# The low part of every fourth weight tile, made by a copy on ACT and an adding transfer

## The chip, the cores and the metric

The kernel runs on one core of a Trainium2 chip. A core has a matrix engine (PE, with a weight loader PEld beside it), a vector engine (DVE), a scalar engine (ACT), a general engine (POOL) and a queue engine (SP). Transfers run on 16 DMA engines, whichever queue issues them; here almost all are issued from SP's queue, and POOL's own queue is used twice. The metric is the device time of one execution in microseconds, smaller is better.

## The reference

The program is a decoder trunk on 256 tokens of width 2048, in float32. There are two layers. The first mixes by latent attention (8 heads) and matrix memory (4 heads) behind one input projection and one output projection; the second by dilated sliding-window attention (16 heads). Each is followed by an MLP of width 8192 with a squared ReLU, and a final RMS norm ends it. Nearly all of the work is products of 256 tokens with weight matrices, some 400 MB of float32 that are each used once.

```
x = x + mix
x = x + squared_relu_mlp(rms_norm(x, norm_mlp[layer]), mlp_w1[layer], mlp_w2[layer])
```

## The kernel before

The matrix engine takes a reduced float32 format, so that every operand is split into a high part of 12 bits and a low part, the rest, and a product is made of three partial products: high by high, high by low, low by high.

The weights come in 769 tiles, counted by `n_w` from 1 in the order of use. `weights` (L93 to L109) makes one: SP issues the transfer of the raw tile (L104), ACT rounds it into `hi` (L107, tile `wh` in the trace), and DVE subtracts (L108, `wl`). Raw, high and low tiles lie in rings of four buffers each, so that tile n uses the buffers of tile n-4. ACT can write `wh` of tile n when PE has done its last product with tile n-4, and DVE then writes `wl`; SP can load the raw tile n+4 when both have read tile n. 716 of the tiles have 128 x 1024 elements (512 KB); those of the input projection at the start are smaller (364, 360 or 344 KB).

`mm_tokens` (L111 to L117) uses a tile with the tokens on the output's partitions: three products for each of two token blocks and each 128 rows, the second of them with the low part. `mm_feats` (L119 to L122) has the features on the partitions: one product of 512 columns with the high part, then one of 256 with the low. So the low part is wanted by the second product of a tile.

The stages in order, with PE's names for their outputs: the input projection of the first layer (`c` tiles 1 to 25, `r`, `qk`, `v`) with the latent heads' projections in between (`un`, `ur`, `uk`, `uv`, one tile each for a pair of heads, four times), its output projection (`o`), the first MLP (tiles 130 to 385: 32 tiles `h`, then 32 tiles `y`, four times), the second layer (`q`, `k`, `v`, `o`), and the second MLP. In its last part (`finish`) the last four tiles are used by products `z` (L863 to L865), for one token block after the other.

The order of the instructions of each engine is made by a planner out of the program's order and its own estimate of times, then fixed; an engine works through its list in order. POOL has little in its list: two norms' powers for whole layers, one for the latents, two in the end, and the transfers of a table (L707) and of the final gain (L828).

Of the kernel before, what the change touches and what calls it, by code (L numbers as in the profile page):

```python
# [14 lines left out]
P = 128  # L15
# [14 lines left out]
def _shape_constants():  # L30
    """Identity, triangles, additive masks and rotary tables: functions of the shapes alone."""
    f = np.float32
    r = np.arange(P)
    ident = np.eye(P, dtype=f)
    cum = (r[:, None] <= r[None, :]).astype(f)
    tri = np.where(r[None, :] <= r[:, None], 0.0, BIG).astype(f)
    zero = np.zeros((P, P), f)
    causal = np.concatenate([tri, zero, tri], 1)
    causal_t = np.concatenate([tri.T, zero, tri.T], 1)

    def log_count(d):
        c = ((d >= 0) & (d <= 128)).astype(int) + ((d >= 0) & (d % 4 == 0)) + ((d >= 0) & (d % 16 == 0))
        return np.where(c > 0, np.log(np.maximum(c, 1)) / DIL_SCALE, BIG).astype(f)

    d0 = r[:, None] - r[None, :]
    dil = np.concatenate([log_count(d0), log_count(d0 + P), log_count(d0)], 1)

    def angles(dim):
        half = dim // 2
        inv = f(THETA) ** (-np.arange(half, dtype=f) * f(2.0) / f(dim))  # L50
        ang = np.arange(S, dtype=f)[:, None] * inv[None, :].astype(f)
        return np.cos(ang), np.sin(ang)

    def by_token(t):
        return t.reshape(NB, P, -1).transpose(1, 0, 2).reshape(P, -1)

    cos, sin = angles(64)
    c64, s64 = by_token(np.concatenate([cos, cos], 1)), by_token(np.concatenate([-sin, sin], 1))
    qc, qs = np.concatenate([cos.T] * 4, 0), np.concatenate([sin.T, sin.T, -sin.T, -sin.T], 0)
    cos, sin = angles(128)  # L60
    oc, os_ = np.concatenate([cos.T, cos.T], 0), np.concatenate([sin.T, -sin.T], 0)
    first = np.concatenate([ident, cum], 1)
    even = np.concatenate([causal, causal_t, c64, s64, qc, qs], 1)
    odd = np.concatenate([dil, oc, os_], 1)
    return tuple(np.ascontiguousarray(t, dtype=f) for t in (first, even, odd))
# [3 lines left out]
def trunk(ctx: ExitStack, tc: tile.TileContext, plan, a, c_first, c_even, c_odd, out):  # L69
# [20 lines left out]

# [1 line left out]
    n_w = [0]  # L92

    def weights(w, k0, kt, c0, n):
        """Rows k0*128.. (kt blocks of 128), columns c0..c0+n (or the ranges c0 of columns, n in all)
        of matrix w -> hi, lo in SBUF.
        The matrix lies in DRAM tile after tile in the order of use: plan says which."""
        name, layer, row = w
        stream, tiles = plan[name, layer]
        at = sum(t[1] * t[3] for t in tiles) * P  # L100
        tiles.append((row + k0 * P, kt, c0 if isinstance(c0, tuple) else ((c0, n),), n))
        n_w[0] += 1
        raw = wpool.tile([P, kt, n], F32, name=f"wr{n_w[0]}", tag="raw", bufs=4)
        nc.sync.dma_start(raw, stream[at:at + P * kt * n].rearrange("(p k n) -> p k n", k=kt, n=n))  # L104
        hi = wpool.tile([P, kt, n], FR, name=f"wh{n_w[0]}", tag="hi", bufs=4)
        lo = wpool.tile([P, kt, n], FR, name=f"wl{n_w[0]}", tag="lo", bufs=4)
        nc.scalar.activation(hi, raw, AF.Copy)  # L107
        nc.vector.tensor_tensor(lo, raw, hi.bitcast(F32), OP.subtract)  # L108
        return hi, lo  # L109

    def mm_tokens(accs, n, T, hi, lo, first, last):  # L111
        """accs[b][:, :n] += T_b.T @ (hi + lo), tokens on the output's partitions."""
        for b in range(NB):
            xh, xl = T[:, 0, b * P:(b + 1) * P], T[:, 1, b * P:(b + 1) * P]
            nc.tensor.matmul(accs[b][:, :n], xh, hi, start=first, stop=False)  # L115
            nc.tensor.matmul(accs[b][:, :n], xh, lo, start=False, stop=False)  # L116
            nc.tensor.matmul(accs[b][:, :n], xl, hi, start=False, stop=last)  # L117

    def mm_feats(ac, T, hi, lo, first, last):  # L119
        """ac[:, :256] + ac[:, 256:] += (hi + lo).T @ T, features on the output's partitions."""  # L120
        nc.tensor.matmul(ac, hi, T.rearrange("p a t -> p (a t)"), start=first, stop=False)  # L121
        nc.tensor.matmul(ac[:, :S], lo, T[:, 0, :], start=False, stop=last)  # L122

    def steps_tokens(Ts, w, c0, n, evac, kt=2, order=None, name="a", split_first=False):
        """Steps (closures) of Ts.T @ w[:, c0:c0+n]; evac(accs) at the end."""
        order = list(order if order is not None else range(len(Ts)))
# [19 lines left out]
    def steps_feats(Ts, w, c0, evac, n=256, name="f"):  # L146
        """Steps of (w[:, c0:c0+n]).T @ Ts; evac(f, acc) for its blocks of 128 features."""
        box = {}
# [18 lines left out]
    def both(pool, out, ac, name):  # L167
        """out = the two halves of a product by features, together."""
        t = pool.tile([P, S], F32, name=f"bt_{name}", tag="bt", bufs=2)
        nc.scalar.activation(t, ac[:, S:], AF.Copy)  # L170
        nc.vector.tensor_add(out, ac[:, :S], t)  # L171

    def rotate(pool, out, y, cos, sin, name):
        """out = y turned: its features i and 64 + i are a pair; sin is negative in the second half."""
        u = pool.tile([P, S], F32, name=f"ro_{name}", tag="ro", bufs=2)
# [6 lines left out]
    def split_to(T, src, scale=None):  # L182
        """T = hi, lo of src * scale (src [128, 256] float32, scale a column or None)."""
        if scale is None:
# [6 lines left out]

# [1 line left out]
    x = [[xpool.tile([P, 512], F32, name=f"x{b}{c}") for c in range(4)] for b in range(NB)]  # L193
# [17 lines left out]

# [1 line left out]
    class Norm:  # L213
# [10 lines left out]
        def load(self, ks):  # L224
            """k-tiles ks (of one pair) from x as it comes, laid out with the features first;
            in the tile that x itself comes into later."""
            n, g, j0 = len(ks), ks[0] // 2, ks[0] % 2
# [19 lines left out]
        def close(self):  # L247
            """mean(x*x) + eps, of a token."""
            s = const.tile([P, NB], F32, name=f"s_{self.name}", tag="s_sum", bufs=2)
            nc.vector.tensor_reduce(s, self.ss, mybir.AxisListType.X, OP.add)  # L250
            nc.vector.tensor_scalar(self.var, s, 1.0 / D, EPS, OP.mult, OP.add)
# [10 lines left out]

# [1 line left out]
    def attn_scores(pool, ps, mask, scale, name):  # L264
        """ps [128, 384]: block 0 x keys 0..127, block 1 x keys 0..255."""
        s = pool.tile([P, 384], F32, name=f"s_{name}", tag="s", bufs=2)
# [27 lines left out]
    def attn_out(pT, v0, v1, name):  # L294
        """out.T [dv, tokens], split: v0, v1 [128 keys, 128]."""
        ps = mis(f"po_{name}")
# [6 lines left out]
    def token_row(pool, column, name):  # L303
        """[128, 256]: a value per token (column [128, block]) along the free axis, on every partition."""
        ps = mis(name)
# [11 lines left out]
    def weave(main, side):  # L317
        """main steps with the side steps spread over them."""
        done = 0
# [18 lines left out]

# [1 line left out]
    def even_layer(norm):  # L340
# [10 lines left out]

        # MLA latents
        cn = big.tile([P, NB, 1088], F32, name="cn", tag="big")
# [57 lines left out]

        # gates and output gate
        gt = sm.tile([P, NB, 8], F32, name="gt")
# [43 lines left out]
        def rows(src, h, name):  # L457
            """[128, 256]: src[:, b, h] of the tokens along the free axis, on every partition."""
            ps = mis(name)
# [36 lines left out]

        # mLSTM queries and keys: convolution over the tokens, channels on partitions
        QK = {}
# [85 lines left out]

        # MLA heads, two at a time
        QT, KT, QR, V = {}, {}, {}, {}
# [113 lines left out]

# [1 line left out]
    def odd_layer(norm):  # L702
# [86 lines left out]

# [1 line left out]
    def two_chunks(T, w, c, evac, ks):  # L791
        """Chunks c, c+1 together, k-tiles outermost."""
        box = {}
# [31 lines left out]
    def finish(H, wq, evac_y, scale, sm):  # L825
        """The last product into x, and the final norm: a block of tokens after the other."""
        gf = sm.tile([P, D], F32, name="gf")
# [172 lines left out]
```

## Time and profile before

| | |
|---|---|
| runs | 2175.34, 2172.87, 2172.86 us; median 2172.87 |
| span of the profiled execution | 2170.5 us |
| PE busy | 2157.0 us, 99% |
| DVE busy | 1317.7 us, 61% |
| ACT busy | 1033.1 us, 48% |
| POOL busy | 5.1 us |
| moved by transfers | 404.49 MB, mean 186 GB/s |
| granted clock | 0.999 of full speed |

The profiled execution is given by its span alone, from the first to the last instruction; the median of the runs is 2.4 us above it. Ends of products are modelled by the profiler, so that PE's rows overlap; where PE waits is read from rows of waits and from the starts of products.

### The profile page before, as it was taken

To read this page: it belongs to the slowest core of one execution; us is meant where nothing else is said; L and a number is where in the kernel's file an instruction comes from. 1 tells how busy PE (TensorE), PEld (TensorE's weight loads), DVE (VectorE), ACT (ScalarE), POOL (GpSimd) and SP (SyncE) were. 2 spreads that over 40 slices of the span, in tenths; PEclk is the share of its full clock that TensorE was granted. 3 is DMA by queue.
4 is the path that set the end of the run, shared out by engine and by line. 5 is a ranking of instruction groups with operands and counts; after the bars stand their busy time and mean duration, and the time that the engine had idled before them with its cause. 6 is when DMAs were issued, how large, how long until landed. Compare 5 with 4: busy or idle time off the path is not lost.

```text
span 2170.5 us, 29176 instructions
## 1 busy us (share of the span) xinstructions
PE 2157.0 (99%) x11214; PEld 1850.6 (85%) x11214; DVE 1317.7 (61%) x1909; ACT 1033.1 (48%) x1476; POOL 5.1 (0%) x11
## 2 busy tenths in 40 slices
PE   9999999999999999999999999999999999999998
PEld 8988888888888888888888888888888888888887
DVE  5668556655654665565667666556546555655655
ACT  6676445443443443444544444455434434434443
POOL 0000000000000000000000000000000000000000
PEclk9999999999999999999999999999999999999999
DMA  8555555555555555555565545555555565555554
GB/s 294 168 164 173 166 180 180 190 193 194 185 188 193 191 185 194 191 188 186 173 201 168 175 165 181 187 185 186 192 192 188 185 194 191 187 193 188 189 189 143
DMA packets 115131, 404.49 MB, mean 186 GB/s; under 512 B 12912, under 2 KB 13552, under 8 KB 114864
## 3 DMA queue, kind: packets, MB, share of 16 engines
q1 hardware_dynamic: 114624, 401.07, 56.7%
q8 instruction: 87, 1.43, 0.3%
q0 software_dynamic: 224, 1.51, 0.2%
q14 instruction: 52, 0.43, 0.1%
q10 hardware_dynamic: 144, 0.06, 0.0%
HBM read 400.49 MB, written 2.10 MB: 185 GB/s over the span
## 4 chain that ended last, share of the span: by engine, by line
PE 98%; ACT 1%; issue 0%; DVE 0%; DMA 0%; SPq 0%; POOLq 0%; POOL 0%; DVEq 0%; ACTq 0%
PE h L121 22%; PE h L122 11%; PE y L115 11%; PE y L117 11%; PE y L116 11%; PE q L121 3%; PE k L121 3%; PE o L117 3%; PE o L115 3%; PE o L116 3%; PE v L115 2%; PE v L117 2%; PE v L116 2%; PE k L122 1%; PE q L122 1%; PE qk L121 1%
## 5 line engine op out<-in xcount | busy, mean ns | idle before, releaser
L108 DVE TENSOR_TENSOR wl<-wr,wh 128x1024 fp32r<-128x1024 f32 (+4 forms) x769 | 922.1, 1200 | 714.6 <-ACT wh L107 709.8
L107 ACT ACTIVATE wh<-wr 128x1024 fp32r<-128x1024 f32 (+4 forms) x769 | 799.3, 1040 | 928.9 <-PE y L117 382.3
L121 PE MATMUL h<-T,wh 128*128 128x512 f32 x2048 | 721.0, 398 | 0.0
L122 PE MATMUL h<-T,wl 128*128 128x256 f32 x2048 | 572.7, 280 | 0.0
L121 PEld LDWEIGHTS h<-T,wh 128*128 128x128 f32 x2048 | 384.6, 188 | 94.1 <-DVE T L189 0.3
L115 PE MATMUL y<-wh,T 128*128 128x512 f32 (+1 forms) x1024 | 395.2, 386 | 0.0
L116 PE MATMUL y<-wl,T 128*128 128x512 f32 (+1 forms) x1024 | 395.0, 386 | 0.0
L117 PE MATMUL y<-wh,T 128*128 128x512 f32 (+1 forms) x1024 | 395.0, 386 | 0.0
L122 PEld LDWEIGHTS h<-T,wl 128*128 128x128 f32 x2048 | 386.3, 189 | 0.4
L117 PEld LDWEIGHTS y<-wh,T 128*128 128x128 f32 x1024 | 192.3, 188 | 38.8
L115 PEld LDWEIGHTS y<-wh,T 128*128 128x128 f32 x1024 | 192.3, 188 | 38.7
L116 PEld LDWEIGHTS y<-wl,T 128*128 128x128 f32 x1024 | 192.3, 188 | 38.4
L115 PE MATMUL o<-wh,T 128*128 128x512 f32 x256 | 102.3, 400 | 0.0
L117 PE MATMUL o<-wh,T 128*128 128x512 f32 x256 | 99.8, 390 | 0.0
L116 PE MATMUL o<-wl,T 128*128 128x512 f32 x256 | 99.6, 389 | 0.0
L170 ACT ACTIVATE bt_h<-h 128x256 f32<-128x256 f32 x128 | 48.7, 381 | 96.8 <-PE h L122 96.8
L121 PE MATMUL q<-T,wh 128*128 128x512 f32 x256 | 92.3, 403 | 0.0
L121 PE MATMUL k<-T,wh 128*128 128x512 f32 x256 | 92.2, 403 | 0.0
L171 DVE TENSOR_TENSOR hu<-h,bt_h 128x256 f32<-128x256 f32 x128 | 54.0, 421 | 44.5 <-ACT bt_h L170 44.5
L115 PE MATMUL v<-wh,T 128*128 128x512 f32 x192 | 77.4, 403 | 0.0
L117 PE MATMUL v<-wh,T 128*128 128x512 f32 x192 | 74.9, 390 | 0.0
L116 PE MATMUL v<-wl,T 128*128 128x512 f32 x192 | 74.8, 390 | 0.0
(261 smaller groups left out, 2018.6 us busy)
## 6 DMA issues: line engine op xcount, KB each, us to landing
wr<-in_mlp_w SPq DMA_DIRECT2D x512, 512.0 KB, 3.5
wr<-in_od_w_qkv SPq DMA_DIRECT2D x96, 512.0 KB, 3.5
wr<-in_ev_w_in SPq DMA_DIRECT2D x32, 512.0 KB, 3.6
wr<-in_ev_w_out SPq DMA_DIRECT2D x32, 512.0 KB, 3.4
wr<-in_od_w_out SPq DMA_DIRECT2D x32, 512.0 KB, 3.5
wr<-in_ev_w_in SPq DMA_DIRECT2D x24, 344.0 KB, 3.2
wr<-in_ev_w_in SPq DMA_DIRECT2D x15, 364.0 KB, 5.7
wr<-in_mla_w_ukv SPq DMA_DIRECT2D x8, 512.0 KB, 3.6
```

The source lines that it names most:

```text
L107: nc.scalar.activation(hi, raw, AF.Copy)
L108: nc.vector.tensor_tensor(lo, raw, hi.bitcast(F32), OP.subtract)
L115: nc.tensor.matmul(accs[b][:, :n], xh, hi, start=first, stop=False)
L116: nc.tensor.matmul(accs[b][:, :n], xh, lo, start=False, stop=False)
L117: nc.tensor.matmul(accs[b][:, :n], xl, hi, start=False, stop=last)
L121: nc.tensor.matmul(ac, hi, T.rearrange("p a t -> p (a t)"), start=first, stop=False)
L122: nc.tensor.matmul(ac[:, :S], lo, T[:, 0, :], start=False, stop=last)
L170: nc.scalar.activation(t, ac[:, S:], AF.Copy)
L171: nc.vector.tensor_add(out, ac[:, :S], t)
```

## The change

In every tile whose number is a multiple of four (192 of 769), the low part is no longer made by DVE. ACT writes the negative of the rounded raw tile into `lo`, and a transfer issued from POOL's queue adds the raw tile to it, read a second time from DRAM. The other tiles are made as before. Comments and docstrings are left out of the file too; the line count shifts by five behind the edit.

```diff
         nc.scalar.activation(hi, raw, AF.Copy)
-        nc.vector.tensor_tensor(lo, raw, hi.bitcast(F32), OP.subtract)
+        if n_w[0] % 4 == 0:
+            nc.scalar.activation(lo, raw, AF.Copy, scale=-1.0)
+            nc.gpsimd.dma_start(lo, stream[at:at + P * kt * n].rearrange("(p k n) -> p k n", k=kt, n=n),
+                                accum_op=OP.add)
+        else:
+            nc.vector.tensor_tensor(lo, raw, hi.bitcast(F32), OP.subtract)
         return hi, lo
```

## Rows read from the trace of the kernel before

**Rows 1.** The page: busy time by engine, and the chain that ended last

```profile
PE 2157.0 (99%) x11214; PEld 1850.6 (85%) x11214; DVE 1317.7 (61%) x1909; ACT 1033.1 (48%) x1476; POOL 5.1 (0%) x11
...
PE 98%; ACT 1%; issue 0%; DVE 0%; DMA 0%; SPq 0%; POOLq 0%; POOL 0%; DVEq 0%; ACTq 0%
```

**Rows 2.** Waits of PEld: in total us, times, longest

```profile
PEld c L115 <- ACT wh L107: 4.9, 3, 4.3
PEld uk L121 <- DVE QT L171: 1.4, 3, 0.8
PEld c L116 <- DVE wl L108: 1.1, 3, 0.5
```

**Rows 3.** Lines: count | busy us, mean ns | idle before, releasers

```profile
L108 DVE TENSOR_TENSOR wl<-wr,wh 128x1024 fp32r<-128x1024 f32 (+4 forms) x769 | 922.1, 1200 | 714.6 <-ACT wh L107 709.8
L107 ACT ACTIVATE wh<-wr 128x1024 fp32r<-128x1024 f32 (+4 forms) x769 | 799.3, 1040 | 928.9 <-PE y L117 382.3 <-issue 195.8 <-PE h L121 131.0
```

**Rows 4.** Timeline (start, duration us) of one y tile, number 190

```profile
512.69 1.06 ACT L107 ACTIVATE wh<-wr 128x1024 fp32r<-128x1024 f32 x1 [1.66 <-PE y L117]
...
520.65 0.39 PE L115 MATMUL y<-wh,T 128*128 128x512 f32 x1
...
520.87 0.39 PE L116 MATMUL y<-wl,T 128*128 128x512 f32 x1
```

**Rows 5.** Timeline of one h tile, number 212, and ACT after the next

```profile
574.04 1.06 ACT L107 ACTIVATE wh<-wr 128x1024 fp32r<-128x1024 f32 x1 [1.76 <-PE h L121]
...
576.93 1.05 ACT L107 ACTIVATE wh<-wr 128x1024 fp32r<-128x1024 f32 x1
...
577.88 0.38 ACT L170 ACTIVATE bt_h<-h 128x256 f32<-128x256 f32 x1
...
582.63 0.28 PE L122 MATMUL h<-T,wl 128*128 128x256 f32 x1
```

**Rows 6.** Timeline around POOL's transfer of the final gain

```profile
1394.12 1.06 ACT L107 ACTIVATE wh<-wr 128x1024 fp32r<-128x1024 f32 x1 [2.01 <-PE o L117]
...
1395.21 1.22 DVE L108 TENSOR_TENSOR wl<-wr,wh 128x1024 fp32r<-128x1024 f32 x1 [1.78 <-ACT wh L107]
1395.30 0.58 POOL L828 DMA_DIRECT2D gf<-in_norm_final  x1 [325.17 <-ACT wh L107]
```

**Rows 7.** Transfers of 1395 to 1400.5 us: queues, issues, us to landing

```profile
q0 software_dynamic: 144, 1.05, 54.3%
q1 hardware_dynamic: 194, 0.73, 32.4%
...
gf<-in_norm_final POOLq DMA_DIRECT2D x1, 1024.0 KB, 5.1
```

**Rows 8.** All 769 loads of raw tiles

```profile
DMA to landing us min/median/max: 2.5/3.5/7.3
```

**Rows 9.** Timeline of tile 4

```profile
9.79 0.82 ACT L107 ACTIVATE wh<-wr 128x728 fp32r<-128x728 f32 x1 [0.70 <-DMA wr<-in_ev_w_in]
...
10.51 0.89 ACT L188 ACTIVATE T<-x,cols 128x256 fp32r<-128x256 f32 x2
...
11.61 0.43 PE L116 MATMUL c<-wl,T 128*128 128x364 f32 x1
```

**Rows 10.** Stretch 10 to 40 us: engines, clock, DMA share, GB/s

```profile
10.00:40.00 30.00, 29.90 (x179) 29.29 (x178) 18.68 (x29) 23.94 (x46) 0.71 (x1) 1.00 0.96 351
```

**Rows 11.** Timeline of tile 24

```profile
45.62 0.81 ACT L107 ACTIVATE wh<-wr 128x720 fp32r<-128x720 f32 x1 [1.16 <-PE c L117]
...
51.48 0.33 PE L116 MATMUL c<-wl,T 128*128 128x360 f32 x1
```

**Rows 12.** Timeline of two of the four uk tiles, numbers 36 and 68

```profile
71.23 1.06 ACT L107 ACTIVATE wh<-wr 128x1024 fp32r<-128x1024 f32 x1 [0.40 <-ACT T L188]
...
77.56 0.28 PE L122 MATMUL uk<-T,wl 128*128 128x256 f32 x1
...
157.78 1.05 ACT L107 ACTIVATE wh<-wr 128x1024 fp32r<-128x1024 f32 x1
...
163.41 0.28 PE L122 MATMUL uk<-T,wl 128*128 128x256 f32 x1
```

**Rows 13.** Timeline of the end, tile 768

```profile
2148.12 1.06 ACT L107 ACTIVATE wh<-wr 128x1024 fp32r<-128x1024 f32 x1 [1.82 <-PE y L117]
...
2153.80 0.28 PE L864 MATMUL z<-wl,T 128*128 128x256 f32 x1
```

## The prediction, written before the changed kernel was run

> **What bounds the kernel now.** I read the page's busy times and its chain first: PE is busy for 2157.0 of 2170.5 us and makes 98% of the chain that ended last [rows 1]. Then the waits: what the weight loader ever waited for DVE's low parts is 1.1 us, all at the start, and its longest wait of all is 4.3 us for the first tile [rows 2]. DVE sits idle for 714.6 us in front of its subtractions, for ACT; ACT sits idle for 928.9 us in front of its roundings, mostly for PE to give a buffer back [rows 3]. So the low parts are early, and DVE's time is worth nothing as such: what matters is how early each low part is, and how much later the changed ones come. That is read tile by tile from timelines, and it differs by stage.
>
> **How early the low part is wanted.** In a y tile ACT starts to round at 512.69, released by PE's last product with the tile four before; PE wants the low part at 520.87 [rows 4]. The changed tile has a second ACT copy of the same size. ACT's next instruction starts 0.95 us after a rounding does (576.93 to 577.88 [rows 5]), so the second copy ends 0.95 after the first: 512.69 + 1.06 + 0.95 = 514.70. From there to 520.87 are 6.2 us. In an h tile: 574.04 + 1.06 + 0.95 = 576.05, wanted at 582.63: 6.6 us [rows 5]. These two stages have 127 of the 192 changed tiles; in each of them the copy and then the whole trip of the adding transfer have to fit in that.
>
> **What is removed.** 192 subtractions of 1.2 us [rows 3], 230 us of DVE time. PE doesn't wait for them, so this is 0. At most it gives back the waits for DVE that are seen: 1.1 + 1.4 us [rows 2], and I take none.
>
> **What is added on ACT.** 192 copies, each holding the queue for some 0.95 us: 182 us, into 928.9 us of idle time. Behind one stands the next rounding, which has 2.7 us until PE frees its buffer. I cost it at 0 by itself; if ACT were full, each copy would cost its 0.95.
>
> **The trip of the adding transfer.** The trace has no adding transfer. The floor is a plain load of a raw tile: 2.5 us at least, 3.5 in the middle; the ceiling that I take from the same row is its longest, 7.3 [rows 8]. The nearest row is POOL's own transfer of the final gain: issued 0.12 us after the rounding that released it had ended (1394.12 + 1.06 = 1395.18, then 1395.30), landed 5.1 us after that [rows 6, 7]. It moved 1.05 MB while loads of raw tiles went on beside it. An adding transfer of 512 KB has to read the raw rows and the rows it adds to, which is also 1.05 MB, so I take 5.1 as a whole, plus 0.1 to start and 0.1 until PE sees it: 5.3 us, between 2.7 and 7.5. On POOL nothing else of length is queued (5.1 us of work in all [rows 1]); behind a waiting transfer stand only a few powers for norms.
>
> The Trainium skill, "Collectives: The Full Stack", section "The bandwidth ceiling: the fold count and why AG ≠ RS ≠ AR", has such an add cost no arithmetic time but two reads on one read ring, which it measured as a rate lower by 1.93. By that rule the trip is the 5.3 us and the sum stays; were the add as cheap as a plain load (3.5 + 0.2 = 3.7 us), all terms below but that of the first tile would go. No row here shows an add.
>
> **Where it doesn't fit.** Steady stages: 5.3 against 6.2 and 6.6, so 0.9 and 1.3 us to spare, cost 0. The others:
> - Tile 4. ACT ends the rounding at 10.61 and is free 0.72 after it started (9.79 to 10.51), so the copy ends at 11.33; plus 5.3 is 16.6, and PE used the low part at 11.61 [rows 9]: 5.0 us late, with no product to put in its place.
> - Transfers at the start. From 10 to 40 us the DMA engines are 0.96 busy at 351 GB/s [rows 10]. Tiles 4, 8, 12, 16 and 20 add five reads of 0.37 MB, 1.9 MB, or 3.7 MB if the rows added to count as well: 5.3 to 10.6 us at that rate. I take 8. The 5.0 us of tile 4 are time in which these engines catch up, so the two aren't added: 8 us for the start together.
> - Tiles 24, 28 and 44, just behind it. Tile 24: 45.62 + 0.81 + 0.72 + 5.3 = 52.45 against 51.48 [rows 11], 1.0 late; with a trip shorter by its smaller size, in time. Half, 0.5 for each: 1.5 us.
> - The four uk tiles, whose roundings come late because ACT is busy with other work. 71.23 + 1.06 + 0.95 + 5.3 = 78.54 against 77.56: 1.0 late; 157.78 + 1.05 + 0.95 + 5.3 = 165.08 against 163.41: 1.7 late [rows 12]; the other two, read in the same way, 0.1 and 0.8. Sum 3.6 us.
> - The end. Tile 768 is the third of four that the first token block runs through in 1.4 us each: 2148.12 + 1.06 + 0.95 + 5.3 = 2155.43 against 2153.80 [rows 13], 1.6 us, with nothing behind it to absorb it.
>
> Sum: 8 + 1.5 + 3.6 + 1.6 = 14.7 us on the span of 2170.5. The median of the runs is 2.4 above that span, so the forecast is 2172.9 + 14.7, about 2188 us. Its own range is 2178 (transfers at the start absorbed, short trips) to 2215.
>
> **Rivals.**
> - The add is slower than two reads, and the trip is longer than the slack of the steady stages. For: no row bounds the add itself, and the changed tiles all use the same one of four buffers, so a late one can't be made up: per four tiles PE loses what the trip is over 6.2 or 6.6 us. At 7.5 us: 63 y tiles by 1.3 and 64 h tiles by 0.9 make 140 us, the 16 o tiles and the 28 of q, k and v with more slack some 10, and the early and last tiles 2.2 more each, some 33 in all with the terms above: 2356 us. Against: the gain's transfer shows that as many bytes land in 5.1. Chance 0.25.
> - The same, much slower (9 us or more). Then every further microsecond costs some 175, and 9 us gives about 2172.9 + 63 x 2.8 + 64 x 2.4 + 44 x 1.4 + 40 = 2605 us. Chance 0.10.
> - DVE holds POOL off from starting the transfer while it subtracts, for up to the 1.2 us of one subtraction: the trip is 6.5, y tiles are 0.3 late (63 x 0.3 = 19 us), the early ones 1.2 more: 2188 + 19 + 10 = 2217 us. Against: the gain's transfer was issued at 1395.30, inside the subtraction of 1395.21 to 1396.43, and its row is 0.58 long [rows 6]. Chance 0.05.
> - Not slower. The mechanism is the start: the transfer there is so short that PE's first tiles don't notice it, and DVE's freed time gives the few waits back. Its place is tile 4, its price 2172.9 - 2.5 = 2170.4 up to 2177, and it decides if the trip at 11.3 us is under 1 us or the lost 5.0 us are made up because the loads were the limit anyway. For: transfers are nearly full there, and PE has just waited for its first tile. Against: PE is busy for 29.90 of those 30 us [rows 10], so there is no wait to hide it in. Chance 0.10.
> - The planner puts transfers behind a long wait in POOL's list, or doesn't make the transfer an add that runs beside the rest; PE then stops once or twice for tens of microseconds: 2220 us and more. Chance 0.03.
>
> The Trainium skill, "SBUF — State Buffer", section "SBUF: two separate sides", speaks for the third of these: a vector operation that uses both of its ports locks POOL out, which then can't write the descriptors of its transfers. The row of the gain speaks against it for this subtraction.
>
> **How the numbers follow.** Forecast 0.47, the rivals 0.25, 0.10, 0.05, 0.10 and 0.03. A measurement of this kernel can't tell less than 0.2%, some 4.3 us, from no change. The range: from 2176, which leaves most of the fourth rival out, to 2450, which takes trips of up to about 8 us in and leaves the second out. Faster 0.03 (the fourth rival at its lowest), within 0.2% 0.10 (the rest of it and the lowest of the forecast), slower 0.87.
>
> **What would show it.** Right: PE's waits for a transfer into the low tiles sum to 10 to 20 us, nearly all before 210 us and at the end; the issues from POOL land in 4.5 to 5.6 us at 512 KB; in the MLPs PE has no wait, and DVE is busy for some 230 us less. Wrong: a wait of PE in every fourth tile of the MLPs, as long as the landing is over 6 us; or no wait at tile 4. A trip over 6.2 us makes the prediction wrong by some 30 us for each half microsecond, and over 6.6 us by some 65.

## The result and the profile after

The changed kernel takes 2347.34 us (median of four runs, 2329.93 to 2355.86) against 2172.86 for the kernel before beside it: 1.079 times as long, 95% interval 1.075 to 1.083. The profiled execution is the run of 2329.93 us, the shortest of the four; its span is 2327.9, 157.4 more than before. The time lies in the range that was given and on the side that was given, but far from the 2188 us that was forecast. It is close to the 2356 us of the first rival.

The page of the kernel after (to be read against [rows 1]):

```profile
PE 2200.7 (95%) x11214; PEld 1854.1 (80%) x11214; DVE 1095.2 (47%) x1717; ACT 1210.1 (52%) x1668; POOL 171.1 (7%) x203
...
PE 16%; DMA 12%; issue 2%; ACT 2%; DVE 0%; ACTq 0%; POOLq 0%; POOL 0%; DVEq 0%
```

DVE is 222 us less busy and ACT 177 us more, near the 230 and 182 of the prediction. The chain that ended last was 98% PE before. Now its shares add up to a third of the span only, so it was not followed further back than that, and transfers stand in it with nearly as much (12%) as PE (16%).

PE's waits (total us, times, longest). Before, PE waited 0.2 us for low parts in all by this view; here it waits for transfers in nearly every stage (the six longest groups):

```profile
PE h L127 <- DMA wl<-in_mlp_w: 49.2, 47, 3.0
PE y L121 <- DMA wl<-in_mlp_w: 14.3, 20, 2.0
PE c L121 <- DMA wl<-in_ev_w_in: 14.3, 6, 7.4
PE uk L127 <- DMA wl<-in_mla_w_ukv: 8.3, 3, 4.4
PE qk L127 <- DMA wl<-in_ev_w_in: 8.1, 2, 5.1
PE v L121 <- DMA wl<-in_ev_w_in: 6.0, 1, 6.0
```

Ends of products are modelled, so these waits are a lower bound. A second measure is the start of the first low product of each tile, after less before. I call it the delay. It grows by 18.4 us up to tile 25, 34.8 more up to tile 129, 55.8 in the first MLP (130 to 385), 11.4 in the second layer's projections, 35.8 in the last MLP and 1.2 behind it. By stage over the whole kernel, h has 64.6 us of it and y 27.0.

The trip of the transfers. First POOL's rows in the MLP (count, busy us, mean ns, idle before), then the issues of transfers in the MLP (KB each, median us to landing; a raw load took 3.5 at the median before [rows 8]):

```profile
L110 POOL DMA_DIRECT2D wl<-in_mlp_w x128 | 110.6, 864 | 1405.5 <-ACT wl L109 1394.6
```

```profile
wr<-in_mlp_w SPq DMA_DIRECT2D x512, 512.0 KB, 4.3
wl<-in_mlp_w POOLq DMA_DIRECT2D x128, 512.0 KB, 7.0
```

The prediction put 5.1 for the 7.0. POOL's issue starts 0.29 us after the copy has ended (median of the 192; the prediction had 0.1), so that from the copy's end to the landing it is 7.3 us in h and 7.4 in y (medians). By the rows of the kernel before the changed tiles had 6.6 and 6.2 us.

A late h tile, number 272, in the timeline after (start, duration, instruction, idle before and releaser; compare [rows 5]):

```profile
828.07 1.06 ACT L107 ACTIVATE wh<-wr 128x1024 fp32r<-128x1024 f32 x1 [3.96 <-PE h L126]
829.03 1.04 ACT L109 ACTIVATE wl<-wr 128x1024 fp32r<-128x1024 f32 x1
830.10 8.96 SPq L104 DMA_DIRECT2D wr<-in_mlp_w  x4
830.37 0.87 POOL L110 DMA_DIRECT2D wl<-in_mlp_w  x1 [12.47 <-ACT wl L109]
...
831.04 0.42 DVE L176 TENSOR_TENSOR hu<-h,bt_h 128x256 f32<-128x256 f32 x1 [5.68 <-ACT bt_h L175]
831.50 0.43 DVE L901 SCALAR_TENSOR_TENSOR hr<-hu 128x256 f32<-128x256 f32 x1
...
838.44 0.39 PE L127 MATMUL h<-T,wl 128*128 128x256 f32 x1 [1.79 <-DMA wl<-in_mlp_w]
```

The rounding waits for PE as before, the copy ends at 830.07, POOL issues at 830.37, and the sum lands 8.0 us later, at 838.37. SP's next raw load goes out at 830.10: the copy is the raw buffer's last reader, so one instruction releases the load and the transfer together, the load 0.27 us ahead.

A y tile, number 192 (compare [rows 4]):

```profile
585.30 1.06 ACT L109 ACTIVATE wl<-wr 128x1024 fp32r<-128x1024 f32 x1 [1.96 <-PE y L121]
586.27 1.04 ACT L107 ACTIVATE wh<-wr 128x1024 fp32r<-128x1024 f32 x1
586.65 0.87 POOL L110 DMA_DIRECT2D wl<-in_mlp_w  x1 [10.54 <-ACT wl L109]
...
593.70 0.19 PEld L121 LDWEIGHTS y<-wl,T 128*128 128x128 f32 x1 [0.25 <-DMA wl<-in_mlp_w]
```

Here the planner put the copy ahead of the rounding, which gives y about 1 us more than the prediction had. With a trip of 7.0 us the weight loader waits 0.25 us for the sum, and y loses less than h.

What the 7 us are, from the transfers' shares in the stretch from issue to landing (queue, packets, MB, share of 16 engines), for tile 192 of the kernel after:

```profile
q0 software_dynamic: 144, 0.52, 47.2%
q1 hardware_dynamic: 287, 1.04, 40.6%
```

47.2% of 7.0 us is 3.3 us on each engine for the transfer itself, and 40.6% is 2.8 us for raw loads in between. The final gain, on which the 5.1 us rested [rows 6, 7], gives from its own issue to its landing:

```profile
q0 software_dynamic: 144, 1.05, 58.5%
q1 hardware_dynamic: 160, 0.59, 28.3%
```

That is 3.0 us for itself and 1.4 us of loads. The transfer's own work was estimated well. The loads beside it were not: there are twice as many. Tile 192 is no exception: over the changed tiles of h and of y the loads take 3.1 us on each engine between issue and landing (medians).

Tile 4 (compare [rows 9]; then three stretches with the same columns as [rows 10]):

```profile
10.51 0.80 ACT L109 ACTIVATE wl<-wr 128x728 fp32r<-128x728 f32 x1
...
11.62 1.02 POOL L110 DMA_DIRECT2D wl<-in_ev_w_in  x1 [11.17 <-ACT wl L109]
...
19.64 0.67 PE L121 MATMUL c<-wl,T 128*128 128x364 f32 x1 [7.37 <-DMA wl<-in_ev_w_in]
```

```profile
10.00:20.00 10.00, 2.60 (x13) 2.31 (x14) 6.59 (x13) 6.60 (x13) 1.02 (x1) 0.73 1.05 350
14.50:267.10 252.60, 215.17 (x1236) 196.51 (x1237) 124.53 (x282) 150.53 (x260) 19.16 (x22) 0.94 0.69 192
267.10:2321.80 2054.70, 1978.68 (x9953) 1652.28 (x9951) 961.50 (x1416) 1047.80 (x1388) 150.57 (x176) 1.00 0.77 219
```

From 10 to 20 us, with that wait in it, the granted clock is 0.73 of full speed, a mix of its two levels, 2.4 and 1.2 GHz; it was 1.00 before [rows 10]. It falls again by the waits in qk, uk and v (0.83 in 200 to 220 us, 0.66 in 260 to 270). At 0.94 over 252.6 us some 30 us are spent at 1.2 GHz, all before 267.1 us. From there to 2321.8 us the clock is 1.00: of the 103.0 us by which the delay grew after tile 129, none is the clock's in this execution. Of the 53.2 us up to tile 129 at most some 15 are, half of those 30 (an estimate).

### The profile page after: what moved, and what is told of

It reads as the page before. It is cut to its first block, busy times and chain, and to the rows that moved or that the text cites. A ratio compares the mean times of both kernels' runs of the same rounds, so it can differ in the third digit from the quotient of the medians.

```text
span 2327.9 us, 29540 instructions
## 1 busy us (share of the span) xinstructions
PE 2200.7 (95%) x11214; PEld 1854.1 (80%) x11214; DVE 1095.2 (47%) x1717; ACT 1210.1 (52%) x1668; POOL 171.1 (7%) x203
## 5 line engine op out<-in xcount | busy, mean ns | idle before, releaser
L113 DVE TENSOR_TENSOR wl<-wr,wh 128x1024 fp32r<-128x1024 f32 (+4 forms) x577 | 691.3, 1199 | 645.2 <-ACT wh L107 640.4
L127 PE MATMUL h<-T,wl 128*128 128x256 f32 x2048 | 580.6, 283 | 50.0 <-DMA wl<-in_mlp_w 49.2
L121 PE MATMUL y<-wl,T 128*128 128x512 f32 (+1 forms) x1024 | 400.4, 391 | 15.0 <-DMA wl<-in_mlp_w 14.3
L109 ACT ACTIVATE wl<-wr 128x1024 fp32r<-128x1024 f32 (+3 forms) x192 | 198.8, 1035 | 191.6 <-PE y L121 117.2
L110 POOL DMA_DIRECT2D wl<-in_mlp_w x128 | 110.6, 864 | 1405.5 <-ACT wl L109 1394.6
L910 DVE SCALAR_TENSOR_TENSOR x<-y,iv_mlp,x 128x512 f32<-128x512 f32 x62 | 44.4, 751 | 81.2 <-PE y L122 81.2
```

The source lines that it names most:

```text
L109: nc.scalar.activation(lo, raw, AF.Copy, scale=-1.0)
L110: nc.gpsimd.dma_start(lo, stream[at:at + P * kt * n].rearrange("(p k n) -> p k n", k=kt, n=n), accum_op=OP.add)
L910: nc.vector.scalar_tensor_tensor(x[b][c], ac[b], scale["s"][:, b:b + 1], x[b][c], OP.mult, OP.add)
```

## The experiments

Theory: the trip of the transfer, from ACT's copy to the landed sum, is longer than the time that the steady stages leave, and each changed tile makes PE wait for the excess. Rivals: the added traffic slows the loads; ACT's copies hold the roundings back; DVE holds POOL off while it works. Times are medians of 4 to 10 runs; the kernel before takes 2173.1 to 2173.8 us beside them. A ratio is to that kernel, with its 95% interval. The diffs are cut to the lines that matter: `src_w` stands for the raw tile's rows in the stream, and `own` holds a pool of buffers that is opened ahead of tile 130, in front of the first MLP.

**Traffic without waiting.** From tile 130 on, all copies and adding transfers, into a buffer that nobody reads.

```diff
+        if own and n_w[0] % 4 == 0:
+            side = own[0].tile([P, kt, n], FR, name=f"ws{n_w[0]}", tag="side", bufs=2)
+            nc.scalar.activation(side, raw, AF.Copy, scale=-1.0)
+            nc.gpsimd.dma_start(side, src_w, accum_op=OP.add)
+        nc.vector.tensor_tensor(lo, raw, hi.bitcast(F32), OP.subtract)
```

> DVE subtracts for every tile as in the kernel before; beside it, for every fourth tile from 130 on, ACT copies and the Pool queue adds raw into a side buffer that nobody reads. Only the traffic and ACT's copies of the later stages are left, with no wait on them. Theory 'waiting for the trip': 2173 to 2180, though raw loads land in about 4.3 us at the median instead of 3.5. Rival 'contention': 2220 to 2290, with PE waiting for low parts made by DVE or for the rounding.

2173.36 us, ratio 1.0001 (0.9991 to 1.0010). The transfers take just as long (page of this kernel, issues; then the longest of PE's waits):

```profile
wr<-in_mlp_w SPq DMA_DIRECT2D x512, 512.0 KB, 4.9
ws<-in_mlp_w POOLq DMA_DIRECT2D x128, 512.0 KB, 6.9
```

```profile
PE c L121 <- ACT wh L108: 4.5, 2, 4.3
PE uk L127 <- DVE QT L177: 0.5, 1, 0.5
PE uk L127 <- DVE qm L513: 0.2, 1, 0.2
```

Raw loads land 1.4 us later than before, and PE doesn't notice. In the steady stages contention costs nothing by itself (at most 0.1% by the interval); only the wait for the result does.

**ACT's copies alone.** All 192 copies, with DVE adding raw to them in place of the transfer.

```diff
-            nc.gpsimd.dma_start(lo, src_w, accum_op=OP.add)
+            nc.vector.tensor_tensor(lo, raw, lo.bitcast(F32), OP.add)
```

> ACT copies minus the raw tile as in the change, but DVE adds raw to it (no Pool-queue transfer); all tiles, the start's too. This prices ACT's 192 copies (1.04 us each, 200 us of ACT) with nothing else. Theory 'the transfer's trip costs': 2173 to 2180, with at most 2 to 5 us at the start. Rival 'ACT's copies hold the roundings back': 2190 or more, and PE waiting for ACT's roundings.

2177.68 us, ratio 1.002 (1.001 to 1.0029). The copies cost some 4 us of 174, so this rival falls too.

**A transfer that doesn't add.**

```diff
-            nc.gpsimd.dma_start(lo, src_w, accum_op=OP.add)
+            nc.gpsimd.dma_start(lo, src_w)
```

> The Pool-queue transfer only writes raw over ACT's copy instead of adding to it; order, waits and the transfer's bytes stay. The low part of every fourth tile is then raw itself, so the sums of those tiles are other numbers. What goes is the second read of each packet (328 ns per 4 KB when it adds, 159 when it does not: 8 packets a queue engine, 2.6 us against 1.3). Theory 'trip too long because the add reads twice': the landing falls from a median of 7.0 us to about 5.0 to 5.5, the waits of h's low products (49 us in all) nearly go, 2180 to 2220. Rival 'Pool queue and its start are what is slow (.86 us of issue, 1.6 to 2.6 us to the first packet), the add is not': landing over 6.2, 2300 to 2350. Rival 'bytes beside the weight loads are what costs': half of the queue's busy time goes, so about half of the 175 us: 2250 to 2270.

2219.88 us, ratio 1.0209 (1.0192 to 1.0226), at the edge of the first theory's range. From this kernel: POOL's rows, the landing, and PE's waits in the MLPs:

```profile
L110 POOL DMA_DIRECT2D wl<-in_mlp_w x128 | 67.5, 528 | 1370.1 <-ACT wl L109 1370.1
```

```profile
wl<-in_mlp_w POOLq DMA_DIRECT2D x128, 512.0 KB, 5.7
```

```profile
PE y L120 <- DMA wl<-in_mlp_w: 2.9, 7, 0.8
PE h L126 <- DMA wl<-in_mlp_w: 2.4, 3, 1.0
```

A packet of 4 KB takes 174 ns here and 328 ns when it adds (medians of all packets of that size on POOL's queue). The issue's row falls from 864 to 528 ns. The landing of 5.7 us mixes two stages that differ: in h it is 4.7 (7.05 when it adds), in y 6.7 (7.04), where the loads take 3.7 us on each engine beside it (medians). In h that fits into the 6.6 us, in y into the 1 us more that the copy ahead of the rounding gives: the delay grows by 15.4 us after tile 129 in place of 103.0. Up to tile 129 24.6 us stay, of 53.2.

**Half of each tile.**

```diff
+            a = kt // 2
+            nc.scalar.activation(lo[:, :a], raw[:, :a], AF.Copy, scale=-1.0)
+            nc.gpsimd.dma_start(lo[:, :a], src_w[:, :a], accum_op=OP.add)
+            nc.vector.tensor_tensor(lo[:, a:], raw[:, a:], hi[:, a:].bitcast(F32), OP.subtract)
```

> Of every fourth tile ACT copies and the Pool queue adds only the first half of its rows (2 KB a partition instead of 4 KB), DVE subtracts the other half. The copy takes about .5 us instead of 1.05 and the queue engines 1.3 us instead of 2.6, so the sum is there some 2 us sooner. Theory 'trip longer than its slack, and bytes make the trip': landing about 5.5, h's excess (median .65 us a changed tile) and y's (.13) are gone, the later stages lose under 15 us instead of 103, the start about 20 to 30 instead of 53: 2190 to 2225. Rival 'a fixed start and end make the trip': landing over 6.3, only ACT's .5 us is won, 2250 to 2310. Rival 'contention': half of the bytes, about 2260.

2197.96 us, ratio 1.0112 (1.0097 to 1.0128). The landing is at 5.3 us, the row on POOL stays 864 ns, and the delay grows by 15.3 us up to tile 129 and 9.3 after it. Half of the bytes take 1.7 us off the trip, not half of it. The transfer's own work falls by 1.5 us on each engine (h, medians), so most of what is gained is that work, as the theory had it.

**A ring of its own, copy first.** Tiles from 130 on.

```diff
+        if own and n_w[0] % 4 == 0:
+            lo = own[0].tile([P, kt, n], FR, name=f"wl{n_w[0]}", tag="la", bufs=2)
+            nc.scalar.activation(lo, raw, AF.Copy, scale=-1.0)
+            nc.gpsimd.dma_start(lo, src_w, accum_op=OP.add)
+            nc.scalar.activation(hi, raw, AF.Copy)
```

> Low parts of every fourth tile from tile 130 on get a ring of their own (two buffers), so ACT's copy and the adding transfer can go ahead of the tile's rounding; tiles before 130 are made as in the kernel before. The same 159 transfers of the later stages, the same bytes and the same adds are there; what goes is the shortage of time between transfer and use. Theory 'PE waits for a trip longer than its slack': issue to use grows by some 4 us in h and y, no low product waits, 2173 to 2185. Rival 'the added reads slow the weight loads or the SBUF for all': the later stages keep their part of the loss (103 us of the 156 us that grew after tile 129, with the clock's part), 2250 to 2290. Rival 'the planner's new order is what costs': 2200 to 2290, with the waits on other tiles.

2265.3 us, ratio 1.0427 (1.041 to 1.0444): a miss for my theory. The waits are those of the third rival. PE's longest waits in this kernel, and what ACT waits for:

```profile
PE y L124 <- DVE wl L116: 19.9, 41, 0.8
PE h L130 <- DVE wl L116: 17.0, 32, 0.8
```

```profile
ACT wl L109 <- DMA wr<-in_mlp_w: 753.4, 127, 9.0
```

PE hardly waits for transfers any more (2.8 us, once). It waits for DVE's low parts of other tiles. The timeline shows why:

```profile
832.33 1.06 ACT L109 ACTIVATE wl<-wr 128x1024 fp32r<-128x1024 f32 x1 [5.50 <-DMA wr<-in_mlp_w]
833.30 1.04 ACT L115 ACTIVATE wh<-wr 128x1024 fp32r<-128x1024 f32 x1
...
834.37 1.23 DVE L116 TENSOR_TENSOR wl<-wr,wh 128x1024 fp32r<-128x1024 f32 x1 [5.72 <-ACT wh L115]
...
835.65 0.50 PE L124 MATMUL y<-wl,T 128*128 128x512 f32 x1 [0.32 <-DVE wl L116]
```

The copy, two tiles ahead, stands at the head of ACT until its raw tile lands. The rounding of an earlier tile is queued behind it, and DVE behind that. This kernel also shows the transfer with almost no load beside it. From the issue at 1054.29 us for 5 us:

```profile
q0 software_dynamic: 144, 0.52, 62.9%
q1 hardware_dynamic: 25, 0.10, 6.8%
```

It works 3.1 us on each engine, as in the changed kernel, with 0.3 us of loads, and lands in 5.2.

**The same, with raw buffers of its own**, so that the copy needn't wait.

```diff
+            raw = own[0].tile([P, kt, n], F32, name=f"wr{n_w[0]}", tag="ra", bufs=2)
```

> As e_early, with the raw tiles of the changed ones in two buffers of their own, so that their loads need not wait for the common four. In e_early the wait for the transfers is gone, but ACT's copy, now two tiles ahead, stands at the head of ACT for its raw tile (753 us idle, 127 times in the MLP), and the next tile's rounding and so DVE's low part come .8 us late (PE waits 19.9 us in y, 17.0 in h). Theory 'ACT held at its head by a raw tile not yet there': those waits fall below 5 us, no low product waits for a transfer, 2173 to 2190. Rival 'ACT copies at another place cost by themselves, whatever they wait for': 2230 to 2270 as in e_early. Rival 'more bytes in flight': loads land later than e_early's 5.8 us and PE waits for roundings, 2200 to 2260.

2176.68 us, ratio 1.0016 (1.0006 to 1.0025). No low product waits for a transfer (PE's waits, complete), though the transfers land later than in the changed kernel:

```profile
PE c L127 <- ACT wh L119: 5.1, 2, 4.3
PE uk L133 <- DVE QT L183: 0.5, 1, 0.5
PE uk L133 <- DVE qm L519: 0.2, 1, 0.2
```

```profile
wl<-in_mlp_w POOLq DMA_DIRECT2D x128, 512.0 KB, 7.5
```

With the time between copy and use made longer, a longer trip makes nothing wait. Some 3.5 us over the kernel before are left; 1.4 of them are there by tile 25, where nothing was changed. This is the best version that was found with the transfers, and it isn't faster than the kernel before, where PE was already 99% busy.

**From tile 130 on alone**, and **every eighth tile**.

```diff
-        if n_w[0] % 4 == 0:
+        if n_w[0] % 4 == 0 and n_w[0] >= 130:
```

> The change for every fourth tile from tile 130 on alone; the start is the kernel before's. If each changed tile pays for itself, the 53 us that the delay grew by up to tile 129 go and the 103 after it stay, with a part of the 16 us of the clock: 2275 to 2290. If the start's delay only shifted the later stages into a worse phase (planned order, transfers on other work): under 2240.

```diff
-        if n_w[0] % 4 == 0:
+        if n_w[0] % 8 == 0:
```

> Every eighth tile instead of every fourth (96 transfers instead of 192). If each changed tile waits for its own trip, about half of the loss: 2250 to 2270. If a stall at one tile gives the next one slack back or a transfer is late because of the one before it: under 2230. If ACT or the queue is saturated by the sum: also under 2230, with a shorter landing than 7.0.

2338.43 us (ratio 1.0757, 1.0716 to 1.0798) and 2299.84 (1.0576, 1.0547 to 1.0606): both above every number that I had given. The start's loss doesn't just add; without it the later stages lose 164 us, not 103. And 96 transfers cost 127 us where 192 cost 174. The landings (first e_late's, then e_mod8's) go with it:

```profile
wl<-in_mlp_w POOLq DMA_DIRECT2D x128, 512.0 KB, 7.4
```

```profile
wl<-in_mlp_w POOLq DMA_DIRECT2D x64, 512.0 KB, 7.7
```

In h alone the last data come 6.6 us after the issue in the changed kernel, 7.5 and 7.8 in these (medians over the transfers), and the delay per changed h tile is 1.0, 1.7 and 2.2 us. A longer trip goes with a longer delay again. The order of the raw loads' issues around the transfers is the same (0.27 us ahead, 2.9 us behind), but the loads take more of each engine's time between issue and landing, 3.6 and 3.9 us in place of 3.1. Whether that lengthens the trip, or the longer trip only meets more loads, is open. A part of these delays is the clock's, unlike the changed kernel's: behind tile 129 their traces have 48 and 31 us at 1.2 GHz, at most 24 and 15 us of delay (an estimate, half of them).

**A load out of the way.** In h the copy reads the rounded tile; the raw buffer is then free 1 us sooner.

```diff
-            nc.scalar.activation(lo, raw, AF.Copy, scale=-1.0)
+            nc.scalar.activation(lo, hi.bitcast(F32) if name == "mlp_w1" else raw, AF.Copy, scale=-1.0)
```

> In the h tiles (first MLP weights) ACT's copy reads the rounded tile instead of raw, with the same value; everything else as in the change. The raw buffer is then free when the rounding ends, 1 us earlier, and the next raw load, which in h is issued .27 us ahead of the adding transfer, goes 1.2 to 1.3 us ahead of it. Theory 'the transfer is slow because the load that the same copy releases goes ahead of it and shares its engines': the first packet comes after about 1.6 us instead of 2.6, the landing in h falls by about 1 us, h's waits (49 us) to under 20, and 2347 to some 2280 to 2300; y is unchanged. Rival 'DVE holds POOL off (hu and hr run while it issues)': lag stays at 2.6 and the time within 10 us of 2347. Rival 'the loads take their turns whenever they come': the first packet is earlier but the last one is not, 2330 to 2350.

And the same in all changed tiles:

> The same for all changed tiles. In y, where the copy stood ahead of the rounding, it must now follow it, so the transfer starts about 1 us later. Theory 'trip against slack': y's waits (14 us) and delay (27 us over 63 changed tiles) grow by up to 63 x 1.0 us, unless the raw load that it meets is out of the way sooner: 2290 to 2360, with h as in the kernel that does it for h alone. Rival 'y is limited by the load issued .68 us behind the transfer': with that load gone ahead, y's landing falls by 1 us too and y's delay stays below 30 us, 2270 to 2295.

2328.24 us (1.0715, 1.0699 to 1.0731) and 2346.5 (1.0806, 1.0788 to 1.0824). Tile 272 in the kernel for h alone:

```profile
824.56 1.06 ACT L107 ACTIVATE wh<-wr 128x1024 fp32r<-128x1024 f32 x1 [2.66 <-PE h L126]
825.65 7.18 SPq L104 DMA_DIRECT2D wr<-in_mlp_w  x3
825.66 1.06 ACT L109 ACTIVATE wl<-wh 128x1024 fp32r<-128x1024 f32 x1
827.01 0.87 POOL L110 DMA_DIRECT2D wl<-in_mlp_w  x1 [11.12 <-ACT wl L109]
```

The load goes 1.36 us ahead now. In h the first packet comes 1.58 us after the issue (median) in place of 2.59, with DVE's `hu` and `hr` beside the issue in both. So DVE was not what held the transfer; the load in front of it was. But the last data come only 0.3 us sooner (6.3 in place of 6.6), and h's delay falls from 64.6 to 54.1 us: the time is near that of the third theory. In the same execution y's delay rises from 27.0 to 36.6 us, though nothing was changed in y, so a stage's delay moves by some 10 us between two kernels on its own, and the fall in h is no more than that. The first packet doesn't set the trip. While a load and the transfer are both under way they take turns (in y some 16 packets of each start in every half microsecond on 16 engines, 173 + 327 ns a pair), so a load that is out of the way early only makes room for the next one. In the kernel that does it everywhere, y's delay rises from 27.0 to 69.8 us over 63 tiles, 0.7 us each, for a copy that must follow its rounding; h's falls to 41.8.

**All kernels together.** In h and in y of the changed kernel and of every experiment with a transfer (medians by stage), the landing is the transfer's own work on each engine, plus that of the loads between issue and landing, plus 0.6 to 1.5 us. With 0.7 us of loads it is 5.3 us (ring of its own), with 3.1 it is 7.0 (the change). This is an account and no forecast, since a longer trip also meets more loads.

## Why the prediction was wrong in size

- Right: DVE's time is worth nothing, and ACT's copies cost some 4 us of 174. The time that the tiles leave was read rightly: 6.6 us in h and 6.2 in y are also the medians over all tiles that were to be changed.
- The step that failed is the trip of the adding transfer, put at 5.3 us, and with it "0.9 and 1.3 us to spare, cost 0". From the copy's end to the landing it is 7.3 us in h and 7.4 in y, the landing alone 7.0. Of the 14.7 us of the sum, all for the ends and the start, none was for the steady stages, where the delay grew by 103 us after tile 129.
- That the time lies in the range is owed to the range's upper part, which was drawn for longer trips, and not to the sum. The first rival (trip 7.5, 2356 us) had the size of the trip but not its reason: the add isn't slower than two reads (the factor is 1.9, below). That its total came out so near is partly luck, since its parts were off in both directions: 140 us for h and y against 91.6, some 33 for the early and last tiles against 54.4 in the profiled execution.
- Why it failed: the gain's transfer was the right row for the transfer's own work (3.0 us on each engine, against 2.9 to 3.3) and the wrong row for the company it kept: 1.4 us of loads on each engine there, 2.8 beside tile 192. With hardly a load beside it, an adding transfer lands in 5.2 us, close to the 5.1 that I took. I had read in [rows 7] that loads were under way and didn't ask whether there were as many as in h and y.
- The Trainium skill, "Collectives: The Full Stack", section "The bandwidth ceiling: the fold count and why AG ≠ RS ≠ AR", has the add of a reduce-scatter cost two reads, a factor of 1.93. The packets' times agree with that factor: 328 ns against 174, 1.9; that it is the second read which takes the time, no run shows. That rule gave the transfer's work, not its trip.
- The slack was off in opposite ways in the two stages. In y the planner put the copy first, 1 us more. In h the copy released the load that goes ahead of the transfer. The order of the first rival's shares is therefore turned round: h 64.6 us, y 27.0, where it had 58 and 82.
- The early terms were too small. Tile 4's transfer landed after 8.0 us and left PE waiting 7.4, and the delay was 18.4 us by tile 25, against 8 for the start and part of 1.5. In qk and v up to tile 97 the planner had ACT do other work between the rounding and the copy (tile 84: rounded at 248.59, copied at 251.70), which no term had. The four uk tiles took 8.4 us, not 3.6; the end 1.2, near the 1.6.
- The third rival falls. In eleven issues of three experiments (5 with the ring of its own, 3 with the half tiles, 3 of the traffic without waiting) a subtraction stood beside POOL's row for more than half a microsecond and no raw load was issued from 0.8 us before to 0.3 us after; the first packet came 1.57 to 1.59 us after the issue (medians of the three), and POOL's row had its usual length. With the half tiles, 81 issues had no DVE work beside POOL's row but a raw load that near, and the first packet came after 2.92 us. The Trainium skill, "SBUF — State Buffer", section "SBUF: two separate sides", has POOL locked out for the whole of a vector operation in a 2-port mode, and of one with two inputs in SBUF only where POOL's operation reads SBUF. It does not count this subtraction, with its two inputs in SBUF, among those that keep POOL from writing descriptors, so it spoke less for this rival than the prediction had it, and these runs show no such lock.
- Open: why the trip in h differs by a microsecond between kernels with the same order of issues, and how much of the delay the clock makes in the runs that weren't profiled.

## What to carry to other kernels

A transfer that takes the place of a computation is to be priced by its trip in the traffic of the stage where it runs: its own packets, and the loads that take turns with them. Compare that with the time between its release and its use, tile by tile; where it doesn't fit, the tile must be started earlier, and every instruction in front of it must be able to start earlier too, or it blocks the engine for what is queued behind it (here 753 us of ACT's time and some 92 us of the kernel's). Look also at what else the releasing instruction sets free.

## What the runs showed of the hardware

- An adding packet of 4 KB takes 328 ns, a writing one 174 on the same queue (medians); POOL's issue takes 864 ns and 528; with half of the bytes an adding issue still takes 864.
- A raw load and an adding transfer that are under way together start as many packets each (16 in half a microsecond on 16 engines, 327 ns and 173 a packet). With 3.1 us of loads on each engine, the transfer's 3.0 to 3.3 us of work land after 7.0 us in the change (medians; 6.3 to 9.3 in h and y).
- Around waits of PE of 4 to 7 us the granted clock is 0.66 to 0.83 over 10 or 20 us. The clock goes with the time of the four runs of the changed kernel, which differ by 26 us: it is 0.992 in the fastest and 0.986 in the slowest, which is some 14 us of 2340 (an estimate).
